# The S5 scan of a four-layer hybrid backbone: 32 groups per scan, products in PSUM, chunk states contiguous

## The chip, the cores and the metric

One core of a Trainium2 chip runs the whole program in one launch. The metric is the device time of a launch in microseconds (us). The engines go by short names: PE is TensorE's matmuls (PEld its weight loads), DVE is VectorE, ACT is ScalarE, POOL is GpSimd, SP issues most DMAs.

## The reference, cut to what matters

Four layers work on 384 tokens of width 1024 in float32: 128 context tokens and 256 latent tokens. Layers 0 and 3 mix tokens with S5, layer 1 with neighbourhood attention, layer 2 with grouped-query attention; every layer ends in a squared-ReLU MLP, and adaLN vectors modulate both halves of a layer. S5 works on 64 groups of 16 channels, with 64 complex states per group and direction:

```python
def s5_scan(ug, ar, ai, abr, abi, bbr, bbi, h0r, h0i, reverse):
    bur = jnp.einsum('gpk,blgk->blgp', bbr, ug)
    bui = jnp.einsum('gpk,blgk->blgp', bbi, ug)
    ...
    _, _, hr, hi = lax.associative_scan(s5_combine, (a_re, a_im, bur, bui), reverse=reverse, axis=1)
    # plus A^n h0 for the latent stream
def s5_mixer(...):
    for dr in range(2):
        hr, hi = s5_scan(ug, ..., reverse=(dr == 1))
        y = y + Re(C h)
        finals.append(the last state)
    z = jax.nn.gelu(y) @ glu_w + glu_b
    za, zg = jnp.split(z, 2, axis=-1)
    return za * jax.nn.sigmoid(zg), finals
```

The context stream starts from zero, the latent stream from `state_s5`; the context's last states are an output.

## The kernel before, in words

**Chunks.** Tokens are cut into 48 chunks of 8: 32 latent ones and 16 of the context. Both directions lie on the partitions: (direction, state) gives 128, and the backward half holds its chunks reversed. The 64 groups go through in 8 batches of 8 (`GB`). S5 has two passes over the batches.

**First pass** (`s5`, the loop over `b` with `s5_states`). For each batch, PE multiplies the chunks with the table E, ACT copies the sums (L1122), PE transposes them (L1129), and ACT copies them into the states' tile `s5s` (L1132 for the 32 latent chunks, L1133 for the 16 of the context). In layer 0 the table E is made on the spot (`make_e`): four DVE multiplications of 128x1024 per batch (`work<-tab,braw`), two POOL sums of 128x1024 (L823, L826), PE transposes. In layer 3 it comes from DRAM, where it was put beside the MLPs of earlier layers. Between the matmuls stand steps of adaLN (`fill`), as long as any are left.

**Scan** (`s5_scan`). After every `SG` = 16 groups, that is after two batches, the recurrence h[c] = A^8 h[c-1] + S[c] runs on DVE over the chunks: 32 steps, of which the first 16 advance both streams (two-stream steps) and the last 16 the latent stream alone (one-stream steps). Each step is three DVE instructions: `scm<-a,s5s` multiplies (128 wide, 64 in a one-stream step), `scm<-scm` adds the products' real and imaginary shares (64, 32), and `s5s<-scm,s5s` adds to S[c] in place (64, 32). Each waits for the one before it. A layer has four scans, each over its 16 groups. POOL copies the context's last states out (L1009).

**Second pass** (`s5_out`). Batch b needs the whole scan of its groups: ACT copies the state before each chunk into `hs` (L1162, four copies), PE multiplies with the table C (L1172) and the chunk's own inputs with the within-chunk table (L1169), ACT applies gelu (L1174). Every second batch, `turn` transposes the result (L1187) and splits it into two exact parts `k` (ACT L1190, DVE `k<-aux,k`). In layer 0 the table C is made here (`make_c`: four DVE multiplications `work<-tab,craw`, POOL sums L874, L877) in the buffers `whi` and `wlo` that otherwise hold weights; in layer 3 it is loaded (`ca`). From batch 4 on, the first half of the GLU's rows is multiplied too (`glu_first`, result `glupart`); after the last batch, `s5_glu` does the second half.

**What sets the order.** A scheduler reads the program and fixes the order of instructions on each engine; engines then run their lists in order and wait on semaphores. So an instruction that waits holds up all that stands behind it in its engine's list. [...]

Of the kernel before, what the change touches and what calls it, by code (L numbers as in the profile page):

```python
# [32 lines left out]
# S5: chunks of Q steps, NC chunk columns (latent 0-15, context 0-15, latent 16-31)  # L33
# [5 lines left out]
# groups per scan; output tiles of the GLU whose first half of the rows comes early  # L39
SG = 16  # L40
# [3 lines left out]
# batches of E and of C of the second S5 layer that are made beside the MLP of a layer  # L44
SPILL = {0: (0, 4), 1: (4, 2), 2: (4, 2)}
# steps of adaLN per step of S5, per projection of the neighbourhood and of the grouped-query attention
FS, FN, FG = 4, 2, 1
# steps of attention per projection
# [3 lines left out]
class Builder:  # L52
# [21 lines left out]
    def psum(self, mm, aux, tab=0, sc=0):  # L74
        """PSUM in banks: sums of projections, all else, tables and scores."""
        if self.ps:
            self.ps.close()
        self.ps = ExitStack()
        self.ps_mm = self.pool(self.ps, f"ps_mm{tab}", mm, space=PSUM)
        self.ps_aux = self.pool(self.ps, f"ps_aux{tab}", aux, space=PSUM)  # L80
        if tab:
            self.ps_tab = self.pool(self.ps, "ps_tab", tab, space=PSUM)
        if sc:
            self.ps_sc = self.pool(self.ps, "ps_sc", sc, space=PSUM)
# [29 lines left out]
    def setup(self):  # L114
# [29 lines left out]
        # the q gains carry the scales of the scores  # L144
# [4 lines left out]
    def streams(self, ap):  # L149
        """The two streams of [P, NTOK]: context columns, latent columns."""  # L150
        return (ap[:, 256:], ap[:, 0:256])

# [21 lines left out]
    def flush(self):  # L174
        """The end of the last group of ada()."""
# [55 lines left out]
    def split(self, pool, src, tag, bufs=None):  # L231
        """src as exact hi + lo."""
# [12 lines left out]
    def proj(self, src, x):  # L245
        """One output tile = chunk^T x over the 8 k-tiles of x."""
# [25 lines left out]
    def scratch(self, start, n):  # L272
        """n values of the space of the norm's parts, where they aren't in use."""
        return self.sc[:, start:start + n]

    def next_norm(self, l, n):
        """The norm that the residual stream goes to next, built up as its tiles become final."""
        self.nx = {"l": l, "n": n, "acc": None, "parts": None, "h": [], "s5": n == 0 and l % 3 == 0}

    def final(self, k):  # L280
        """x[k] is final: x gain as exact parts, the shifts in two more columns, or as chunks for S5; and the sum of
        squares."""
# [37 lines left out]
    def rstd(self):  # L320
        """1 / rms of every token, on all partitions."""
# [6 lines left out]
    def normed(self, pool, ps, r, func, dst):  # L328
        """dst = func(r * ps + shift) from a projection of the parts that final() makes."""
# [9 lines left out]
    def rsqrt(self, m, r):  # L339
        """(m + EPS)^-1/2: a first value from the tables, one Newton step."""  # L340
# [12 lines left out]
    def pick(self, out, gg, src):  # L353
        """out[(step, channel)] = src(step)[channel of group gg], steps in reverse."""
# [5 lines left out]
    def residual(self, ps, gate, f):  # L360
        """x[f] += gate * ps."""
# [3 lines left out]
    def out_proj(self, src, half, x, l, steps, fill):  # L365
        """x += gate * (W^T o) over half of the heads."""
# [64 lines left out]
    def head_rstd(self, pool, raws, kind):  # L431
        """1 / rms over the head dim of up to four raw [P, NTOK] tiles."""
# [9 lines left out]
    def head_norm(self, raw, r, j, gain, kind, t):  # L442
        """t = raw r gain, r that of the j-th tile."""
# [7 lines left out]
    def pipeline(self, items):  # L451
        """Pairs of functions, of which the first runs one ahead: steps that other work is interleaved with."""
# [7 lines left out]
    def steps(self, n):  # L460
        """n steps of the attention that runs beside the projections, and the fill of adaLN."""
# [11 lines left out]
    def value_flip(self, raws, v, first):  # L473
        """v[tok, t, feature] from features by tokens."""
# [3 lines left out]
    def softmax_tail(self, p, total):  # L478
        """p *= 1 / total."""
# [3 lines left out]
    def flip(self, p, n, dst):  # L483
        """dst[key, n, q] = transposes of p [q, n * P]."""
# [117 lines left out]
    def gqa(self, l):  # L602
        nc, i = self.nc, self.i
        with ExitStack() as ctx:
# [13 lines left out]
            def project(first, n, st):  # L618
                """The tiles of k (2) and q (8): projected, then normed, turned and used in steps."""
# [90 lines left out]
    def exp(self, pool, out, x):  # L710
        """exp(x) by 2^n e^r, x within float32's range of exponents."""
# [40 lines left out]
    def s5_tables(self, tp, wide, slot, pe, pc, a8):  # L752
        """Discretised parameters: powers of the step in the order of each direction, for E with B's factor; the matrix of
        Q steps. wide: space for 34 G values."""
# [21 lines left out]
        # f = (A - 1) / lambda  # L776
# [14 lines left out]
        # the order of the steps: the first 64 partitions run forward  # L791
# [16 lines left out]
    def make_e(self, pool, slot, b, pe, work, kf, kp, dd, et):  # L808
        """E[(step, channel), g, r, (direction, state)] = A^j B of GB groups, steps in reverse; and into DRAM the
        products Re(C A^j B) within a chunk, one row of 16 values per (distance, channel)."""  # L810
# [24 lines left out]
        # two groups per product, of which the diagonal blocks count  # L835
# [28 lines left out]
    def make_c(self, cr, b, pc, ca, t):  # L864
        """ca = (Re, -Im) of C A^j."""
# [13 lines left out]
    def s5_spill(self, slot, first, ebs, cbs):  # L879
        """The tables of a later S5 layer, kept in DRAM: steps that other work is interleaved with. The parameters come  # L880
        first, then E and C of some groups."""
# [55 lines left out]
    def s5(self, l, slot):  # L937
# [5 lines left out]
        # places in the scratch space: what final() makes, then the reversed chunks of the second half and y; sel;  # L943
        # the reversed chunks of the first half, then the states that y is made from; kp and d, or sums of states
# [5 lines left out]
        with ExitStack() as ctx:  # L950
# [3 lines left out]
            s = []  # L954
            for n in range(2):
                t = pool.tile([P, HG // SG, NC + 2, 2, SG], F32, name=f"s5s{n}", tag=f"s5s{n}")
                s += [t[:, m] for m in range(HG // SG)]
            for n, t in enumerate(s):
                nc.gpsimd.dma_start(t[:, 0], i["s5h0"][slot][:, :, n * SG:(n + 1) * SG])
                nc.gpsimd.memset(t[:, 33], 0.0)  # L960
# [24 lines left out]
            for b in range(NB):  # L985
# [20 lines left out]
                if not g:  # L1006
                    gg = slice((n - 1) * SG, n * SG)
                    self.s5_scan(pool, s[n - 1], a8[:, :, :, gg])
                    nc.gpsimd.tensor_copy(fin[:, :, gg], s[n - 1][:, NC + 1])  # L1009
# [49 lines left out]
    def s5_u(self, pool, u, make=None):  # L1059
        """u[(step, channel), g, chunk], steps in reverse: from x's chunks in layer 0, from those of x gain else."""  # L1060
# [45 lines left out]
    def s5_states(self, ssb, b, et, u, ur, s):  # L1106
        """S[c] = sum over the steps of a chunk of A^j B u for GB groups (columns 48-63 of a group belong to the next)."""
# [16 lines left out]
        def rest():  # L1124
            for n in range(GB // 4):
                pt = self.aux().rearrange("p (j r e c) -> p j r e c", r=2, e=2, c=CP)
                for j in range(2):
                    for r in range(2):
                        nc.tensor.transpose(pt[:, j, r].rearrange("p e c -> p (e c)"), sums[2 * n + j][:, r, :], self.ident[:])  # L1129
                for r in range(2):  # L1130
                    dst = s[:, :, r, gs + 4 * n:gs + 4 * n + 4].rearrange("p c (j e) -> p j e c", e=2)
                    nc.scalar.copy(dst[:, :, :, 1:33], pt[:, :, r, :, 0:32])  # L1132
                    nc.scalar.copy(dst[:, :, :, 34:], pt[:, :, r, :, 32:NC])  # L1133
        return rest

    def s5_scan(self, pool, s, a8):
        """h[c] = A^Q h[c - 1] + S[c] in place: the first value of each stream, then its chunks (latent from 0, context
        from 33); the backward half holds them in reverse."""
        w0 = s.shape[3]
        m = pool.tile([P, 2, 2, 2, w0], F32, name="scm", tag="scm", bufs=2)  # L1140
        for n in range(32):
            if n < 16:
                cur, prev = s[:, n + 1:n + 35:33], s[:, n:n + 34:33]
            else:
                cur, prev = s[:, n + 1:n + 2], s[:, n:n + 1]
            w = cur.shape[1]
            sh = [P, w, 2, 2, w0]
            self.mul(m[:, :w], a8.unsqueeze(1).to_broadcast(sh), prev.unsqueeze(2).to_broadcast(sh))
            self.add(m[:, :w, :, 0], m[:, :w, :, 0], m[:, :w, :, 1])
            self.add(cur, m[:, :w, :, 0], cur)  # L1150

    def s5_out(self, pool, b, ca, tz, u, s, hy, gsb, k):
        """The outputs of GB groups: from the state before each chunk and from the chunk itself."""
# [3 lines left out]
        for dr in range(2):  # L1157
            pp = slice(64 * dr, 64 * dr + 64)
            hv = hy[pp].rearrange("p g r c -> p c r g")
            for a0, n, src in ((0, 32, 0), (32, 16, 33)):  # L1160
                dst = hv[:, a0:a0 + n]
                nc.scalar.copy(dst if dr == 0 else dst[:, ::-1], sg[pp, src:src + n])  # L1162
# [32 lines left out]
    def glu_sums(self, slot, f, halves, k):  # L1195
        """Both output tiles of f over halves of the rows."""
# [181 lines left out]
```

## Time and profile before

| what | value |
|---|---|
| runs | 2102.32, 2106.98, 2116.06 us, median 2106.98 |
| span of the profiled execution | 2104.6 us |
| median minus that span | 2.4 us |
| busy: PE, DVE, ACT, POOL | 94%, 65%, 49%, 10% of the span |
| S5 of layer 0 | first output matmul at 149.8 us, last at 241.0 |
| S5 of layer 3 | first output matmul at 1714.4 us, last at 1778.0 |

The profiled execution has no time of its own beside the span; the runs' median lies 0.1% above it. In a list of groups, the first column is the source line; element-wise DVE instructions share the helper's line L93, so their tiles tell them apart. `128x64` is partitions by elements per partition. PEclk is the clock granted to PE, as a share of full speed.

### The profile page before, as it was taken

The page shows a single profiled execution, that of the slowest core. Times are in us where ns is not written, and L with a number is a line of the kernel's source. Part 1 is how long each engine was busy: PE and PEld are TensorE (multiplying, and loading weights), DVE is VectorE, ACT ScalarE, POOL GpSimd, SP SyncE. Part 2 cuts the span into 40 slices and gives each one's busy share as a digit, 9 for nine tenths or more (in the row PEclk, how much of TensorE's full clock was granted, in tenths as well). Part 3 has the DMA queues.
Part 4 walks back from the last instruction along what each step waited for, and adds up shares of the span by engine and source line. Part 5 has one row for each costly group of instructions (what it writes and reads, how often), then busy time and mean ns, then how long its engine had stood idle before and what let it go on. Part 6 is the DMA issues. An engine that isn't in the chain of part 4 may idle for free. (4 is left out here: it accounts for less than half of the span.)

```text
span 2104.6 us, 35187 instructions
## 1 busy us (share of the span) xinstructions
PE 1980.7 (94%) x13490; PEld 1747.3 (83%) x13490; DVE 1368.2 (65%) x3070; ACT 1029.4 (49%) x2112; POOL 216.4 (10%) x180
## 2 busy tenths in 40 slices
PE   5886899999999999999999999999999878999999
PEld 2554799999987777998999877998997657999999
DVE  7899669856445556856658566856665396674562
ACT  4664656335355555634435555534434477553441
POOL 4443210400000000001111000002111000000000
PEclk8997999999999999999999999999999999999999
DMA  7756654443365555634334532533444575333331
GB/s 286 234 199 238 233 182 152 152 170 120 128 233 192 177 179 193 230 121 154 125 132 163 172 114 98 179 131 128 142 149 156 165 281 221 121 126 125 124 131 67
DMA packets 130823, 348.45 MB, mean 166 GB/s; under 512 B 12800, under 2 KB 48544, under 8 KB 128608
## 3 DMA queue, kind: packets, MB, share of 16 engines
q1 hardware_dynamic: 124160, 338.55, 46.8%
q0 software_dynamic: 1712, 4.05, 0.6%
q10 hardware_dynamic: 4784, 3.61, 0.5%
q8 instruction: 107, 1.75, 0.3%
q14 instruction: 60, 0.49, 0.1%
HBM read 323.22 MB, written 22.94 MB: 164 GB/s over the span
## 5 line engine op out<-in xcount | busy, mean ns | idle before, releaser
L221 ACT CAST whi<-raw 128x1024 fp32r<-128x1024 f32 x340 | 356.4, 1049 | 486.4 <-PE mm L228 422.6
L93 DVE TENSOR_TENSOR wlo<-raw,whi 128x1024 fp32r<-128x1024 f32 x340 | 445.2, 1310 | 197.2 <-ACT whi L221 196.3
L227 PE MATMUL mm<-h,whi 128*128 128x386 f32 x1312 | 453.4, 346 | 0.0
L229 PE MATMUL mm<-h,wlo 128*128 128x386 f32 x1312 | 448.2, 342 | 0.0
L228 PE MATMUL mm<-h,whi 128*128 128x386 f32 x1312 | 446.9, 341 | 0.0
L227 PE MATMUL mm<-ahi,whi 128*128 128x384 f32 x1024 | 350.2, 342 | 10.3 <-ACT ahi L235 10.3
L229 PE MATMUL mm<-ahi,wlo 128*128 128x384 f32 x1024 | 349.3, 341 | 2.8 <-DVE wlo L93 2.8
L228 PE MATMUL mm<-alo,whi 128*128 128x384 f32 x1024 | 349.8, 342 | 1.7 <-DVE alo L93 1.6
L227 PEld LDWEIGHTS mm<-h,whi 128*128 128x128 f32 x1312 | 246.7, 188 | 21.7 <-issue 16.7
L228 PEld LDWEIGHTS mm<-h,whi 128*128 128x128 f32 x1312 | 248.3, 189 | 5.0 <-issue 3.7
L229 PEld LDWEIGHTS mm<-h,wlo 128*128 128x128 f32 x1312 | 247.4, 189 | 5.3 <-issue 4.0
L111 DVE SCALAR_TENSOR_TENSOR x<-mm,mod,x 128x128 f32<-128x128 f32 (+1 forms) x256 | 95.4, 412 | 204.8 <-PE mm L229 204.3
L227 PEld LDWEIGHTS mm<-ahi,whi 128*128 128x128 f32 x1024 | 195.3, 191 | 13.3 <-ACT ahi L235 12.6
L229 PEld LDWEIGHTS mm<-ahi,wlo 128*128 128x128 f32 x1024 | 195.3, 191 | 5.0 <-DVE wlo L93 3.4
L228 PEld LDWEIGHTS mm<-alo,whi 128*128 128x128 f32 x1024 | 195.2, 191 | 5.1 <-DVE alo L93 5.1
L163 PE MATMUL ada<-raw,silu 128*2 128x256 f32 x1536 | 127.1, 407 | 21.1 <-DMA raw<-in_ada_w 16.5
L93 DVE TENSOR_TENSOR nt<-mm,rstd 128x384 f32<-128x384 f32 x164 | 90.6, 553 | 68.1 <-PE mm L229 67.5
L337 ACT ACTIVATE relu<-nt,nb 128x128 f32<-128x128 f32 (+1 forms) x256 | 102.1, 447 | 46.3 <-DVE nb L335 45.9
L235 ACT CAST ahi<-asq 128x384 fp32r<-128x384 f32 x128 | 65.4, 513 | 119.2 <-DVE asq L93 118.8
L93 DVE TENSOR_TENSOR alo<-asq,ahi 128x384 fp32r<-128x384 f32 x128 | 73.0, 572 | 50.3 <-ACT ahi L235 50.2
L163 PEld LDWEIGHTS ada<-raw,silu 128*2 128x2 f32 x1536 | 31.4, 85 | 77.4 <-issue 32.2
L227 PE MATMUL mm<-k,whi 128*128 128x384 f32 x256 | 89.1, 352 | 6.0 <-DVE k L93 2.1
(376 smaller groups left out, 3019.1 us busy)
## 6 DMA issues: line engine op xcount, KB each, us to landing
raw<-in_w SPq DMA_DIRECT2D x256, 512.0 KB, 3.5
raw<-in_ada_w SPq DMA_DIRECT2D x192, 512.0 KB, 4.7
raw<-in_glu SPq DMA_DIRECT2D x32, 512.0 KB, 5.5
tz<-kdr SPq DMA_DIRECT2D x16, 512.0 KB, 5.8
dca<-ca SPq DMA_DIRECT2D x8, 1024.0 KB, 4.3
raw<-in_na_wqk SPq DMA_DIRECT2D x16, 512.0 KB, 4.1
det<-et SPq DMA_DIRECT2D x32, 256.0 KB, 2.6
et<-det SPq DMA_DIRECT2D x32, 256.0 KB, 5.7
```

Source lines behind the costliest of these rows:

```text
L93: self.nc.vector.tensor_tensor(out, a, b, op=op)
L111: self.nc.vector.scalar_tensor_tensor(out, a, s, b, op0=op0, op1=op1)
L163: nc.tensor.matmul(ps[32 * j:32 * j + 2], self.silu[:, k, :], raw[:, 256 * j:256 * j + 256], start=(k == 0), stop=(k == KT - 1))
L221: nc.scalar.copy(hi[:], raw[:])
L227: mm(out, whi, xhi, start=first, stop=False)
L228: mm(out, whi, xlo, start=False, stop=False)
L229: mm(out, wlo, xhi, start=False, stop=last)
L235: self.nc.scalar.copy(hi[:], src)
L337: nc.scalar.activation(o, z, func, bias=b[:, s:s + 1])
```

## The change

`SG` goes from 16 to 32: a layer has two scans of 32 groups, the first after batch 3, the second after batch 7. Each step still has three DVE instructions, of twice the width. The multiplication (256 wide, 128 in a one-stream step) writes its products to a PSUM bank `m`, which the scan keeps to its end; two additions (128, 64) then take the products' two shares from PSUM one after the other and add each straight to S[c] in SBUF. In layer 3 `m` is an `sc` bank; in layer 0 the first scan takes one of the three `aux` banks, the second one of the two `mm` banks. The 48 chunks lie at 0 to 47 of the states' tile and the two start values at 48 and 49, so that a batch's S come in by two ACT copies (L1129, 128x384) in place of eight, and leave `s5_out` by five copies (64x752, 64x496, 64x240 and two of 64x32) in place of four. The copy of the last context states, L1008, still needs only the first 16 steps. Four DMAs and four memsets of start values on POOL, ahead of S5, go.

```diff
-SG = 16
+SG = 32
...
-            s = []
-            for n in range(2):
-                t = pool.tile([P, HG // SG, NC + 2, 2, SG], F32, name=f"s5s{n}", tag=f"s5s{n}")
-                s += [t[:, m] for m in range(HG // SG)]
+            s = [pool.tile([P, NC + 2, 2, SG], F32, name=f"s5s{n}", tag=f"s5s{n}") for n in range(2)]
             for n, t in enumerate(s):
-                nc.gpsimd.dma_start(t[:, 0], i["s5h0"][slot][:, :, n * SG:(n + 1) * SG])
-                nc.gpsimd.memset(t[:, 33], 0.0)
+                nc.gpsimd.dma_start(t[:, NC], i["s5h0"][slot][:, :, n * SG:(n + 1) * SG])
+                nc.gpsimd.memset(t[:, NC + 1], 0.0)
...
-                    self.s5_scan(pool, s[n - 1], a8[:, :, :, gg])
-                    nc.gpsimd.tensor_copy(fin[:, :, gg], s[n - 1][:, NC + 1])
+                    m = self.scores() if sp else (self.aux, self.mm_tile)[n - 1]()
+                    self.s5_scan(m, s[n - 1], a8[:, :, :, gg])
+                    nc.gpsimd.tensor_copy(fin[:, :, gg], s[n - 1][:, NC - 1])
...
-                pt = self.aux().rearrange("p (j r e c) -> p j r e c", r=2, e=2, c=CP)
+                pt = self.aux().rearrange("p (r j m) -> p r j m", r=2, m=P)
...
-                for r in range(2):
-                    dst = s[:, :, r, gs + 4 * n:gs + 4 * n + 4].rearrange("p c (j e) -> p j e c", e=2)
-                    nc.scalar.copy(dst[:, :, :, 1:33], pt[:, :, r, :, 0:32])
-                    nc.scalar.copy(dst[:, :, :, 34:], pt[:, :, r, :, 32:NC])
+                nc.scalar.copy(s[:, 0:NC, :, gs + 4 * n:gs + 4 * n + 4].rearrange("p c r g -> p r g c"),
+                               pt.rearrange("p r j (e c) -> p r (j e) c", c=CP)[:, :, :, 0:NC])
...
-        m = pool.tile([P, 2, 2, 2, w0], F32, name="scm", tag="scm", bufs=2)
+        m = m[:, :8 * SG].rearrange("p (w a r g) -> p w a r g", a=2, r=2, g=SG)
         for n in range(32):
...
             self.mul(m[:, :w], a8.unsqueeze(1).to_broadcast(sh), prev.unsqueeze(2).to_broadcast(sh))
-            self.add(m[:, :w, :, 0], m[:, :w, :, 0], m[:, :w, :, 1])
-            self.add(cur, m[:, :w, :, 0], cur)
+            for r in range(2):
+                self.add(cur, m[:, :w, :, r], cur)
...
-            for a0, n, src in ((0, 32, 0), (32, 16, 33)):
-                dst = hv[:, a0:a0 + n]
-                nc.scalar.copy(dst if dr == 0 else dst[:, ::-1], sg[pp, src:src + n])
+            if dr == 0:
+                nc.scalar.copy(hv[:, 1:NC], sg[pp, 0:NC - 1])
+            else:
+                nc.scalar.copy(hv[:, 30::-1], sg[pp, 0:31])
+                nc.scalar.copy(hv[:, 46:31:-1], sg[pp, 32:47])
+            first, gap = ((0, 32), (31, 16))[dr]
+            nc.scalar.copy(hv[:, first:first + gap + 1:gap], sg[pp, NC:NC + 2])
```

In the changed kernel the lines move a little: the copies into the states' tile are L1129, those out of it L1155 to L1160, the output matmuls L1167 and L1170, gelu L1172.

**DVE, layer 3, kernel before**, where the first scan of a tile has reached its one-stream steps. `s5s_16539` is the tile that holds the first two scans; a width of 2x32 is a two-stream step, 32 a one-stream step.

```order
L93 TENSOR_TENSOR scm<-a_16550,s5s_16539 128x128
L93 TENSOR_TENSOR s5s_16539<-scm,s5s_16539 128x2x32
L93 TENSOR_TENSOR scm<-scm 128x4x16
L93 TENSOR_TENSOR scm<-a_16550,s5s_16539 128x64
L93 TENSOR_TENSOR s5s_16539<-scm,s5s_16539 128x2x32
L93 TENSOR_TENSOR scm<-scm 128x2x16
L93 TENSOR_TENSOR scm<-a_16550,s5s_16539 128x128
L93 TENSOR_TENSOR s5s_16539<-scm,s5s_16539 128x32
```

**The same place in the changed kernel.** `s5s_16299` holds the first scan (batches 0 to 3), `s5s_16300` the second (4 to 7); `x2` is the two additions of a step.

```order
L93 TENSOR_TENSOR sc<-a_16306,s5s_16299 128x256
L93 TENSOR_TENSOR s5s_16299<-sc,s5s_16299 128x2x64 x2
L93 TENSOR_TENSOR s5s_16300<-sc,s5s_16300 128x2x64
L93 TENSOR_TENSOR sc<-a_16306,s5s_16299 128x128
L93 TENSOR_TENSOR s5s_16300<-sc,s5s_16300 128x2x64
L93 TENSOR_TENSOR s5s_16299<-sc,s5s_16299 128x64
L93 TENSOR_TENSOR sc<-a_16306,s5s_16300 128x256
L93 TENSOR_TENSOR s5s_16299<-sc,s5s_16299 128x64
```

In both, two scans alternate. Before, these are scans over batches 0 and 1 and over 2 and 3. In the changed kernel the first scan's 16 two-stream steps stand by themselves (the first two rows repeat), then the second scan's first addition, which needs the copies of batch 7 among others, stands ahead of the first scan's 16 one-stream steps, and the two alternate from there.

**ACT, layer 3, changed kernel**, from the copies of the last two batches to the first gelu.

```order
L1129 COPY s5s_16300<-aux 128x2x4x48
L1158 COPY hs<-s5s_16299 64x15x2x8
L221 CAST whi<-raw 128x1024 x4
L1157 COPY hs<-s5s_16299 64x31x2x8 x2
L1155 COPY hs<-s5s_16299 64x47x2x8 x2
L1160 COPY hs<-s5s_16299 64x2x2x8 x2
L1172 ACT_TABLE_LOAD
L1172 ACTIVATE hs<-aux 128x4x8x16
```

The copies out of the states' tile that need the end of the first scan (L1157 and L1155, of batches 0 and 1) stand after the last copy into it; before, six copies out of it (L1162) stood ahead of the last batch's copies into it.

**DVE, layer 0, changed kernel**, where the first scan starts. `work<-tab,braw` is E, `mod` adaLN; `aux` holds the products.

```order
L93 TENSOR_TENSOR work<-tab,braw 128x1024 x13
L93 TENSOR_TENSOR mod_2_975<-aux,ab 128x8 x2
L93 TENSOR_TENSOR work<-tab,braw 128x1024 x8
L93 TENSOR_TENSOR aux<-a_159,s5s_148 128x256
L93 TENSOR_TENSOR s5s_148<-aux,s5s_148 128x2x64 x2
```

Before, a first scan started after batch 1, with E's multiplications between its steps. Now 28 of the 32 multiplications of E stand ahead of the first scan; the other four and ten of the table C's stand among its steps, and the second scan begins in the first one's eighth one-stream step.

## Rows read from the trace of the kernel before

**Rows 1.** the page, engines: busy us (share of the span) and instructions

```profile
PE 1980.7 (94%) x13490; PEld 1747.3 (83%) x13490; DVE 1368.2 (65%) x3070; ACT 1029.4 (49%) x2112; POOL 216.4 (10%) x180
```

**Rows 2.** windows, layer 0: window, its us, busy us by engine, PEclk, DMA

```profile
100.00:125.00 25.00, 21.27 (x244) 12.59 (x230) 25.00 (x93) 16.85 (x57) 9.69 (x9) 1.00 0.62 223
...
175.00:200.00 25.00, 14.14 (x122) 8.35 (x122) 25.00 (x76) 6.42 (x14) 10.42 (x7) 0.66 0.59 205
200.00:225.00 25.00, 21.05 (x203) 17.52 (x204) 23.22 (x58) 15.09 (x26) 9.60 (x4) 0.93 0.74 247
```

**Rows 3.** windows, layer 3, columns as in rows 2

```profile
1714.30:1731.00 16.70, 11.40 (x155) 9.58 (x154) 14.53 (x88) 14.79 (x21) 0.21 (x1) 0.95 0.76 268
1731.00:1743.00 12.00, 9.19 (x68) 7.43 (x68) 9.20 (x59) 3.86 (x7) 0.68 (x2) 0.78 0.51 186
1743.00:1767.00 24.00, 23.81 (x204) 22.36 (x205) 17.37 (x62) 19.68 (x26) 0.08 (x1) 0.93 0.67 258
1767.00:1782.00 15.00, 12.05 (x113) 9.64 (x110) 4.43 (x12) 8.50 (x23) 0.00 (x0) 1.00 0.55 199
```

**Rows 4.** groups, VectorE, 97.5 to 235 us: shapes, count | busy us, mean ns

```profile
L93 DVE TENSOR_TENSOR work<-tab,craw 128x1024 f32<-128x1024 f32 x32 | 38.7, 1213 | 0.8 <-PE aux L1172 0.5 <-issue 0.3
L93 DVE TENSOR_TENSOR scm<-a,s5s 128x64 f32<-128x64 f32 x64 | 25.8, 421 | 0.2
L93 DVE TENSOR_TENSOR scm<-scm 128x32 f32<-128x32 f32 x64 | 25.6, 406 | 0.1
L93 DVE TENSOR_TENSOR scm<-a,s5s 128x128 f32<-128x128 f32 x57 | 18.7, 356 | 0.0
L93 DVE TENSOR_TENSOR s5s<-scm,s5s 128x32 f32<-128x32 f32 x64 | 11.5, 183 | 0.1
...
L93 DVE TENSOR_TENSOR k<-aux,k 128x192 fp32r<-128x192 f32 x12 | 6.1, 510 | 0.0
...
L93 DVE TENSOR_TENSOR mod<-aux,ab 128x8 f32<-128x8 f32 x12 | 1.9, 159 | 0.0
L111 DVE SCALAR_TENSOR_TENSOR gain<-mod,ng 128x8 f32<-128x8 f32 x4 | 0.6, 160 | 0.0
```

**Rows 5.** groups, GpSimd, 0 to 260 us, columns as in rows 4

```profile
L874 POOL TENSOR_TENSOR work<-work 128x1024 f32<-128x1024 f32 x8 | 19.1, 2391 | 34.5 <-DVE work L93 19.4 <-DVE s5s L93 10.0 <-DVE scm L93 5.1
```

**Rows 6.** timeline, VectorE, layer 0: start us, us, line, operation, tiles

```profile
112.13 2.58 DVE L93 TENSOR_TENSOR scm<-a,s5s 128x64 f32<-128x64 f32 x2
```

**Rows 7.** timeline, GpSimd, the same stretch

```profile
112.12 2.45 POOL L823 TENSOR_TENSOR work<-work 128x1024 f32<-128x1024 f32 x1 [3.06 <-DVE s5s L93]
```

**Rows 8.** timeline, VectorE, layer 3, two-stream steps (at the end: idle before, releaser)

```profile
1690.28 0.29 DVE L93 TENSOR_TENSOR scm<-a,s5s 128x128 f32<-128x128 f32 x1
1690.61 0.22 DVE L93 TENSOR_TENSOR scm<-scm 128x64 f32<-128x64 f32 x1
...
1691.62 0.23 DVE L93 TENSOR_TENSOR s5s<-scm,s5s 128x64 f32<-128x64 f32 x1 [0.20 <-ACT s5s L1133]
1691.76 0.22 DVE L93 TENSOR_TENSOR scm<-scm 128x64 f32<-128x64 f32 x1
```

**Rows 9.** timeline, VectorE, layer 3, one-stream steps of the last scan alone

```profile
1757.57 0.19 DVE L93 TENSOR_TENSOR scm<-scm 128x32 f32<-128x32 f32 x1
...
1760.64 0.19 DVE L93 TENSOR_TENSOR s5s<-scm,s5s 128x32 f32<-128x32 f32 x1
```

**Rows 10.** timeline, ScalarE, layer 3, around the first output

```profile
1713.73 0.36 ACT L1133 COPY s5s<-aux 128x64 f32<-128x64 f32 x1
1714.12 2.25 ACT L1162 COPY hs<-s5s 64x512 f32<-64x512 f32 x2
```

**Rows 11.** output matmuls, layer 3: ns min/median/max, first and last start us

```profile
L1172 PE MATMUL aux<-ca,hs x256: 272/273/450, 1714.4 to 1778.0; 128*48 128x128 f32 x128
```

**Rows 12.** output matmuls, layer 0, columns as in rows 11

```profile
L1172 PE MATMUL aux<-work,hs x256: 272/273/448, 149.8 to 241.0; 128*48 128x128 f32 x128
```

**Rows 13.** timeline, ScalarE, layer 0, end of the copies of batch 3

```profile
97.49 0.32 ACT L1133 COPY s5s<-aux 128x64 f32<-128x64 f32 x1
```

More of the change, by code (lines that the diff above doesn't have):

```diff
@@ L1125, in rest, with s5_scan @@
             for n in range(GB // 4):
-                pt = self.aux().rearrange("p (j r e c) -> p j r e c", r=2, e=2, c=CP)
+                pt = self.aux().rearrange("p (r j m) -> p r j m", r=2, m=P)
                 for j in range(2):
                     for r in range(2):
-                        nc.tensor.transpose(pt[:, j, r].rearrange("p e c -> p (e c)"), sums[2 * n + j][:, r, :], self.ident[:])
-                for r in range(2):
-                    dst = s[:, :, r, gs + 4 * n:gs + 4 * n + 4].rearrange("p c (j e) -> p j e c", e=2)
-                    nc.scalar.copy(dst[:, :, :, 1:33], pt[:, :, r, :, 0:32])
-                    nc.scalar.copy(dst[:, :, :, 34:], pt[:, :, r, :, 32:NC])
-        return rest
-    def s5_scan(self, pool, s, a8):
-        w0 = s.shape[3]
-        m = pool.tile([P, 2, 2, 2, w0], F32, name="scm", tag="scm", bufs=2)
+                        nc.tensor.transpose(pt[:, r, j], sums[2 * n + j][:, r, :], self.ident[:])
+                nc.scalar.copy(s[:, 0:NC, :, gs + 4 * n:gs + 4 * n + 4].rearrange("p c r g -> p r g c"),
+                               pt.rearrange("p r j (e c) -> p r (j e) c", c=CP)[:, :, :, 0:NC])
+        return rest
+    def s5_scan(self, m, s, a8):
+        m = m[:, :8 * SG].rearrange("p (w a r g) -> p w a r g", a=2, r=2, g=SG)
         for n in range(32):
[L1142 to L1147, printed above, removed]
+            w = 2 if n < 16 else 1
+            at = lambda c: s[:, c:c + 32 * w - 31:32] if w > 1 else s[:, c:c + 1]
+            cur, prev = at(n), at(n - 1) if n else s[:, NC:NC + 2]
+            sh = [P, w, 2, 2, SG]
             self.mul(m[:, :w], a8.unsqueeze(1).to_broadcast(sh), prev.unsqueeze(2).to_broadcast(sh))
-            self.add(m[:, :w, :, 0], m[:, :w, :, 0], m[:, :w, :, 1])
-            self.add(cur, m[:, :w, :, 0], cur)
+            for r in range(2):
+                self.add(cur, m[:, :w, :, r], cur)
     def s5_out(self, pool, b, ca, tz, u, s, hy, gsb, k):
```

## The prediction

> **What bounds the kernel now.** The page's engines come first: PE is busy for 94% of the span, DVE for 65% [rows 1]. So a DVE saving counts only in a stage where PE waits for DVE. S5 is the only part that the change touches, so the next view is the windows of its two layers. In layer 0 DVE is busy for 25.00 us of 25 in four windows from 100 to 200 us, of which the first and last stand here, while PE falls to 14.14 of 25 at a granted clock of 0.66 [rows 2]: this stage is bound by DVE. In layer 3 PE is busy for 11.40 + 9.19 + 23.81 + 12.05 = 56.5 us of the 67.7 us from the first output matmul, at 1714.4, to 1782 [rows 3, 11]; 11.2 us are gaps. The groups on DVE in layer 0 say what fills it: scans, then the tables of C, 32 x 1.21 us [rows 4]. The timelines then give the price of one step of a scan [rows 8, 9] and what releases the first output [rows 10].
>
> **Instructions of a scan.** A step's three instructions wait for each other, so a scan alone pays each duration and a gap: 1690.28 + 0.29 = 1690.57, and the next starts at 1690.61, a gap of 0.04; where two scans alternate, the next starts after 0.14 (1691.62 to 1691.76) although 0.23 is its duration, that is 0.08 to 0.09 earlier than it ends [rows 8]. Durations: 128 wide 0.29, 64 wide 0.22 [rows 8], 32 wide 0.19 [rows 9]. From 64 to 128 is 1.1 ns an element, so I estimate 0.43 for 256 wide. Per 32 groups:
> - before, two scans alternating: two-stream pair of steps 2 x (0.21 + 0.14 + 0.14) = 0.98, one-stream 2 x (0.14 + 0.11 + 0.11) = 0.72; 16 of each, 27 us.
> - after, hidden among other work: 0.35 + 2 x 0.21 = 0.77 and 0.21 + 2 x 0.14 = 0.49; 16 of each, 20 us.
> - after, alone: 0.47 + 2 x 0.33 = 1.13 and 0.33 + 2 x 0.26 = 0.85; 16 of each, 32 us.
>
> So the change saves 7 us of DVE per 32 groups where other work fills the gaps, and costs 5 where nothing does. What fills them is the order of the instructions.
>
> **The PSUM operand.** No row shows DVE writing to PSUM. A read from PSUM costs nothing in the nearest row, `mod<-aux,ab` at 159 ns against 160 for `gain<-mod,ng` from SBUF; the far end is `k<-aux,k`, 510 ns at 192 wide where 64 and 128 wide at 0.22 and 0.29 would give 0.36, so 0.15 dearer [rows 4, 8]. I take nothing, by the short instructions, which are nearest in length; nothing excludes a gain, which I bound by the surplus below. [...]
>
> **Layer 3.** Before, the first scans were long done when batch 7's copies into the states ended (1713.73 + 0.36 = 1714.09), and the first output matmul came at 1714.4 [rows 10, 11]. Now:
> - The first scan starts when batch 3's copies are in, as before at 1691.62, where DVE's idle time ends on ACT's copy [rows 8]. Its 16 two-stream steps stand alone: 16 x 1.13 = 18, to 1709.6.
> - The second scan's first addition stands next in DVE's list and waits for batch 7's copies. Two copies in place of eight save ACT under 1 us, so about 1713.
> - 16 steps of both, 0.49 + 0.77 = 1.26 each, 20 us: the first scan ends at 1733.
> - ACT's copies out follow. Two of 64x512 took 2.25 [rows 10], so by size 64x496 takes about 1.1 and 64x752 about 1.65; two of L1157 and two of L1155 (5.5) stand ahead of the first small one. Output starts at about 1738.
>
> That is 24 us later than 1714.4, and PE has nothing else in its list there. Part of it comes back: before, PE waited on later scans (the last ended at 1760.64 + 0.19 [rows 9]), now the second ends at 1733 + 16 x 0.85 = 1747, ahead of the output that needs it. PE's 56.5 us of work [rows 3] put the end at 1794.5 without a gap, 12.5 after 1782, and at 24 later with all gaps kept. The idle stretch may lower PE's clock, which stood at 0.78 behind the gaps of 1731 to 1743 [rows 3], and a stretch without gaps may raise it, so I count neither. I take +13: the gaps were waits for scans and copies, and these are over by then.
>
> **Layer 0.** DVE's list is shorter. The scans' instructions are lengthened here: one-stream multiplications take 421 ns in place of 220 and first additions 406 in place of 190, two-stream multiplications 356 in place of 290 [rows 4, 8, 9]: 64 x 0.20 + 64 x 0.22 + 57 x 0.07 = 31 us. Where from: a pair of multiplications takes 2.58 us from 112.13 to 114.71 while POOL's sum runs from 112.12 to 114.57 [rows 6, 7]. The tables of C, with one source in PSUM, stay at 1213, and POOL's sums take 2.39 [rows 4, 5]. After, the additions have one source in PSUM, and only the multiplications have two in SBUF; since DVE works in order, POOL's sum may still catch the next multiplication. I keep half of the 31, and bound it by none and by all. So DVE saves 2 x 7 + 15 = 29 us at best, and about 25 with some steps alone.
>
> Against it stands the late start. Batch 3's copies end at 97.81 [rows 13], and 28 tables of E stand ahead of the first scan, so I start it at 102. 16 steps of 1.13, eight other tables (9.7, which fill some gaps) and 8 us of POOL lead to about 137; eight one-stream steps, six tables and 4 us of POOL (0.85 x 8 + 7.3 + 4 = 18) to 155; eight joint steps of 1.26 to 165. With copies out, output starts at about 167 against 149.8 [rows 12]. Then DVE has left the rest of the second scan (7 x 0.9 + 16 x 0.6 = 16), 22 tables (25, at 1.14 start to start), POOL 8, and the rest 10: 59, to 226, and about 7 more to the last output matmul: 233 against 241.0 [rows 12]. PE's own work in that stretch is, by the mean of the last two windows (17.6 of 25) [rows 2], 64 of its 91 us, so its floor is 167 + 64 = 231. I take -4, half of the 8, since neither engine will go without gaps. The two held PSUM banks make `aux` two for batches 4 to 7, and `mm` one until the second scan ends; the GLU, which needs both `mm`, starts after that anyway. I price them at nothing, at up to +8 for the range (2 us for each of four batches).
>
> **The sum.** 2104.6 (the profiled span) + 13 - 4 = 2113.6; the median lies 2.4 above the span, so **2116**. The ACT copies saved and the DMAs on POOL lie beside other work; if ACT were on the path in the first pass, they would give 1 us a batch.
>
> **The rivals.**
> - *Forecast* (0.50): layer 3 pays, layer 0 gives a little back: 2103 to 2127.
> - *Layer 0 gains fully* (0.22). The stall goes with the products, DVE loses all 31 us, the first scan ends ten earlier, and and PE's floor is 157 + 64 = 221: -20 at most, -15 with some gaps. Layer 3 still pays 6 to 13: 2093 to 2105; were it to pay nothing, 2085 to 2092. For it: DVE's full windows and the 2.58 us [rows 2, 6]. Against: the multiplications keep two SBUF sources.
> - *Late outputs pass through* (0.20), slower. The mechanism is layer 3's first scan, which ends only after batch 7's copies: where the gaps of 11.2 us return behind the late start (copies out of ACT being the pace, five a batch in place of four), the delay of 24 stays, layer 0 gives 0: 2131. It decides from 19 us net on. For it: PE's list holds nothing else meanwhile. Against: the last scan, which ended at 1760.83, is over sooner [rows 9].
> - *PSUM operands dearer* (0.08): by the far end of 0.15, 48 + 96 instructions with one in layer 3's path add up to 20 us there, of which half may come back, and 10 in layer 0: 2126 to 2146.
>
> About 1% (21 us) is what a measurement here can tell from no change. Below 2086: the low case of layer 0's full gain with nothing paid in layer 3, 0.10. Above 2128: most of the third and half of the last, 0.22. Within: 0.68. The range leaves out one tenth at each side: 2092 to 2134.
>
> **What would show it.** In the profile after: L1129's last copy in layer 3 at about 1713 and the first output matmul at 1738 on the old time axis, with PE empty between; the first scan's steps at 1.1 us alone and 1.26 in pairs; PE nearly full from then on. In layer 0: additions from PSUM near 0.22 and 0.29 without a long tail, multiplications with a tail up to 2.4; first output at 160 to 170, last at 230 to 240. Wrong would be: additions from PSUM above 0.35, a first output in layer 3 before 1730, or an output in layer 0 after 245.

## The result

The changed kernel takes 2124.57 us (median of 4 runs, 2122.01 to 2130.14), the kernel before 2107.07 on the same chip: a ratio of 1.0088, 95% interval 1.0066 to 1.0109. It is 17.5 us slower. The forecast was 2116 in a range of 2092 to 2134.

The page's line of engines, which answers to [rows 1]: DVE lost 38 us of busy time, and the program got longer.

```profile
PE 1974.4 (93%) x13490; PEld 1735.5 (82%) x13490; DVE 1330.2 (63%) x2686; ACT 1032.1 (49%) x2032; POOL 212.2 (10%) x168
```

**Where the time went.** All kernels here cast 340 weight chunks in the same order (`whi<-raw`), so the starts of these casts divide a profile into stages: to the 9th cast (layer 0's S5), to the 257th (the middle layers), to the 281st (layer 3's S5). From there to the last cast it is 249.0 us in every kernel, and to the end 269.8. "First output" is the time from the start of layer 3's stage to its first output matmul. Each number below is read from the trace of the one profiled execution.

| kernel | layer 0 | middle | layer 3: first output | layer 3 whole |
|---|---|---|---|---|
| before | 258.4 | 1343.0 | 113.1 | 233.5 |
| changed | 257.0 | 1341.7 | 132.5 | 253.5 |

Layer 0 gave 1.4 us, the middle 1.3, and layer 3 took 20.0, on spans of 2104.6 and 2122.0.

**Layer 3.** Output matmuls of the changed kernel (first and last start), against 1714.4 and 1778.0 in [rows 11]; the stage began 2.7 us earlier:

```profile
L1170 PE MATMUL aux<-ca,hs x256: 272/273/450, 1731.2 to 1794.8; 128*48 128x128 f32 x128
```

The windows ahead of the first output and behind it (columns as in [rows 3]): PE is empty for 22.5 us, then busy for 55.52 of 67.8 us, where [rows 3] have 56.5 of 67.7. PE's granted clock stands at its lower level (0.50) in the hole, yet behind it the mean is 0.91, against 0.92 by the windows of [rows 3].

```profile
1708.70:1731.20 22.50, 0.02 (x2) 0.03 (x2) 22.50 (x102) 9.19 (x11) 0.85 (x2) 0.50 0.27 109
1731.20:1799.00 67.80, 55.52 (x533) 49.12 (x533) 24.39 (x68) 42.74 (x76) 0.00 (x0) 0.91 0.57 195
```

The waits of PE between 1700 and 1800 (total, times, longest) name a single one for that hole; `L1160` is the last of the copies out of the states' tile:

```profile
PE aux L1170 <- ACT hs L1160: 22.5, 1, 22.5
PE aux L1185 <- DVE s5s L93: 5.7, 1, 5.7
```

Two timelines, DVE and then ACT, show what the copies waited for. The first scan's two-stream steps alone start 1.11 us apart (1687.69 to 1688.80: a multiplication of 0.43, two additions in 0.62). They end at 1704.41. DVE then idles 3.81 us for batch 7's copies, which end at 1708.18, and the joint steps follow at 1.20 us each (1709.61 to 1710.81).

```profile
1687.69 0.43 DVE L93 TENSOR_TENSOR sc<-a,s5s 128x256 f32<-128x256 f32 x1
1688.15 0.62 DVE L93 TENSOR_TENSOR s5s<-sc,s5s 128x128 f32<-128x128 f32 x2
1688.80 0.43 DVE L93 TENSOR_TENSOR sc<-a,s5s 128x256 f32<-128x256 f32 x1
...
1703.79 0.62 DVE L93 TENSOR_TENSOR s5s<-sc,s5s 128x128 f32<-128x128 f32 x2
1708.21 0.29 DVE L93 TENSOR_TENSOR s5s<-sc,s5s 128x128 f32<-128x128 f32 x1 [3.81 <-ACT s5s L1129]
...
1709.61 0.29 DVE L93 TENSOR_TENSOR sc<-a,s5s 128x128 f32<-128x128 f32 x1
...
1710.81 0.29 DVE L93 TENSOR_TENSOR sc<-a,s5s 128x128 f32<-128x128 f32 x1
```

```profile
1707.38 0.80 ACT L1129 COPY s5s<-aux 128x384 f32<-128x384 f32 x1
...
1726.27 1.92 ACT L1157 COPY hs<-s5s 64x496 f32<-64x496 f32 x2 [10.90 <-DVE s5s L93]
1728.21 2.85 ACT L1155 COPY hs<-s5s 64x752 f32<-64x752 f32 x2
```

The copies out start at 1726.27, when the first scan's last step but one is done, and 4.9 us later PE starts.

**Layer 0.** Output matmuls, against 149.8 and 241.0 in [rows 12], the scans' groups from 97.5 to 235 us, against [rows 4], and two windows, against [rows 2]:

```profile
L1170 PE MATMUL aux<-work,hs x256: 272/273/421, 164.4 to 241.2; 128*48 128x128 f32 x128
```

```profile
L93 DVE TENSOR_TENSOR aux<-a,s5s 128x256 f32<-128x256 f32 x16 | 11.2, 700 | 0.4
L93 DVE TENSOR_TENSOR mm<-a,s5s 128x256 f32<-128x256 f32 x16 | 10.2, 640 | 0.0
L93 DVE TENSOR_TENSOR mm<-a,s5s 128x128 f32<-128x128 f32 x16 | 9.5, 595 | 0.4
L93 DVE TENSOR_TENSOR s5s<-aux,s5s 128x128 f32<-128x128 f32 x32 | 9.3, 289 | 1.3 <-ACT s5s L1129 0.4
...
L93 DVE TENSOR_TENSOR s5s<-aux,s5s 128x64 f32<-128x64 f32 x32 | 6.8, 212 | 0.2
L93 DVE TENSOR_TENSOR aux<-a,s5s 128x128 f32<-128x128 f32 x16 | 6.6, 413 | 0.1
```

```profile
150.00:175.00 25.00, 16.66 (x211) 9.22 (x205) 19.72 (x65) 15.32 (x22) 6.59 (x3) 0.80 0.91 312
...
200.00:225.00 25.00, 13.78 (x155) 10.17 (x154) 13.82 (x35) 10.86 (x17) 2.35 (x1) 0.80 0.62 207
```

The scans are much cheaper: with the two groups of `mm` additions left out here (8.9 and 7.1 us) they are busy for 69.6 us; four of the six groups before alone took 81.6 [rows 4]. Additions with one source in PSUM stay at 289 and 212 ns; the multiplications, with two in SBUF, are lengthened, at 700 ns where layer 3's take 430. DVE, full in all of 100 to 200 us before, now has gaps. Yet output starts 14.6 us later and ends at 241.2.

### The profile page after: what moved, and what is told of

It reads as the page before. It is cut to its first block, busy times and chain, and to the rows that moved or that the text cites. A ratio compares the mean times of both kernels' runs of the same rounds, so it can differ in the third digit from the quotient of the medians.

```text
span 2122.0 us, 34660 instructions
## 1 busy us (share of the span) xinstructions
PE 1974.4 (93%) x13490; PEld 1735.5 (82%) x13490; DVE 1330.2 (63%) x2686; ACT 1032.1 (49%) x2032; POOL 212.2 (10%) x168
## 5 line engine op out<-in xcount | busy, mean ns | idle before, releaser
L163 PE MATMUL ada<-raw,silu 128*2 128x256 f32 x1536 | 133.1, 414 | 39.0 <-DMA raw<-in_ada_w 25.3
## 6 DMA issues: line engine op xcount, KB each, us to landing
det<-et SPq DMA_DIRECT2D x32, 256.0 KB, 2.7
et<-det SPq DMA_DIRECT2D x32, 256.0 KB, 5.7
```

Of the source, the lines that this page charges most:

```text
L163: nc.tensor.matmul(ps[32 * j:32 * j + 2], self.silu[:, k, :], raw[:, 256 * j:256 * j + 256], start=(k == 0), stop=(k == KT - 1))
```

## The experiments

Ratios are to the kernel before, in runs on the same chip. The stages of all experiments, in us:

| kernel | ratio (95% interval) | layer 0 | middle | layer 3: first output | layer 3 whole |
|---|---|---|---|---|---|
| l0_32 | 1.0027 (1.0009 to 1.0046) | 254.5 | 1345.9 | 115.2 | 238.4 |
| l3_32 | 1.0152 (1.0125 to 1.0179) | 266.4 | 1348.4 | 133.0 | 255.2 |
| both16 | 1.0079 (1.0049 to 1.0108) | 264.8 | 1346.2 | 115.4 | 238.4 |
| sbuf | 1.0128 (1.0100 to 1.0155) | 264.0 | 1342.1 | 129.9 | 251.5 |
| share3 | 1.0115 (1.0094 to 1.0136) | 257.5 | 1354.0 | 128.4 | 253.1 |
| old32 | 1.0055 (1.0036 to 1.0075) | 253.2 | 1347.2 | 129.6 | 249.4 |
| layout16 | 1.0051 (1.0033 to 1.0069) | 261.9 | 1346.6 | 113.6 | 238.6 |
| mix | 0.9998 (0.9979 to 1.0017) | 257.2 | 1348.2 | 110.7 | 229.8 |
| tail_cut | 1.0104 (1.0086 to 1.0122) | 256.7 | 1345.0 | 133.7 | 253.2 |
| ada_after | 1.0115 (1.0095 to 1.0135) | 254.6 | 1344.6 | 131.4 | 253.7 |
| ada_before | 1.0022 (1.0008 to 1.0036) | 256.0 | 1340.1 | 110.1 | 237.8 |
| ada_mix | 1.0043 (1.0026 to 1.0060) | 258.8 | 1342.6 | 108.0 | 237.4 |

The same code of a stage differs by up to 4 us between kernels in layer 0 (254.5 to 258.8 in the six other kernels that have the changed kernel's layer 0) and in layer 3 (233.5 before, 229.8 in mix), and by more in the middle, where none of these kernels is changed (the last section has the reason). So stages are compared, and differences under 4 us are not read.

### Which layer, and is it the grouping

**l0_32**, 32 groups in layer 0 only (`SGS` gives the groups for layers 0 and 3; the edits here are cut to the lines that matter):

```diff
-SG = 32
+SGS = (32, 16)
```

> Two scans of 32 groups in layer 0, four of 16 in layer 3; products in PSUM and the contiguous layout in both. Theory A (layer 3's late first output is the whole loss): layer 3 comes back to its time before, so 2100 to 2108 us, within 0.4% of the kernel before. Rival B (the loss is in what both layers share: PSUM products, five copies out in place of four): about half of the 17 us stays, 2113 to 2118.

2114.3 us, ratio 1.0027. Theory A and rival B each hold in part: 15 of layer 3's 20 us are gone, but it stays 5 above the kernel before.

**l3_32**, 32 groups in layer 3 only. In layer 0 two scans of 16 share a PSUM bank, one half each:

```diff
-SG = 32
+SGS = (16, 32)
...
-                    m = self.scores() if sp else (self.aux, self.mm_tile)[n - 1]()
+                    if sp:
+                        m = self.scores()
+                    elif SG == 32:
+                        m = (self.aux, self.mm_tile)[n - 1]()
+                    elif n % 2:
+                        bank = (self.aux, self.mm_tile)[n // 2]()
+                        m = bank
+                    else:
+                        m = bank[:, 256:]
```

> Four scans of 16 groups in layer 0, two of 32 in layer 3; products in PSUM and the contiguous layout in both. Theory A: layer 3 starts its output some 22 us late as in the changed kernel and ends about 20 late, layer 0 is at or below its time before, so 2115 to 2127 us. Rival B: half the loss, 2113 to 2118, with layer 0 losing as much as layer 3.

2141.5, outside what either theory gave. Layer 3's loss is 22 us, as theory A has it; the surprise is layer 0, at 266.4, 8 us worse than before and some 10 worse than with 32 groups.

**both16**, with `SGS = (16, 16)` and the same banks:

> Four scans of 16 groups in both layers, products in PSUM, contiguous layout. Theory A (grouping alone costs): no loss; layer 3 -3 us by the fewer copies in, layer 0 -3 to -12 as additions from PSUM no longer wait for GpSimd: 2092 to 2104 us. Rival B (PSUM and layout cost): slower than before by 8 us or more.

2126.2: theory A fails for the whole kernel, and the time is where rival B put it. Layer 3 has the 5 us again, first output 2 us late and the rest slower. PE's wait ahead of the first output ends on a copy out of the states, which had no such share before:

```profile
PE aux L1183 <- ACT hs L1173: 4.3, 1, 4.3
```

In layer 0 the trace shows the two scans of a bank one after the other: the first one's last multiplication starts at 129.1 us, the second one's first at 130.0, where the kernel before ran such scans side by side. That is likely a cost of this kernel's own way to place products; layout16 (below), which does not share banks, has 261.9 in layer 0, so it is not shown to be all of the 6 to 8 us.

**layout16**, 16 groups with products in SBUF, three instructions of `scm` as before, only the new layout:

```diff
-SG = 32
+SGS, PSM, OLD, SHARE = (16, 16), (0, 0), (False, False), (0, 0)
...
+                    if not PSM[slot]:
+                        m = pool.tile([P, 8 * SG], F32, name="scm", tag="scm", bufs=2)
...
+            if not direct:
+                self.add(m[:, :w, :, 0], m[:, :w, :, 0], m[:, :w, :, 1])
+                self.add(cur, m[:, :w, :, 0], cur)
+                continue
```

(By layer: `PSM`, products in PSUM, which `s5_scan` gets as `direct`; `OLD`, the old layout; `SHARE`, one bank for both scans.)

> Four scans of 16 groups, products in SBUF as before, and only the contiguous layout with its two copies in and five copies out. Theory F: layer 3 ends 4 to 5 us late by the copies out, layer 0 about as before: 2110 to 2116 us. Rival G (the layout also costs layer 0 its 7 us, and not the bank that two scans shared in the kernel with 16 groups and PSUM products): 2118 to 2128.

2120.1, in rival G's range, but the stages do not bear G out: layer 0 is 3.5 above before, within what is not read, and not 7; the unchanged middle adds 3.6. Layer 3 is again at 238.6, so the 5 us there belong to the layout and not to PSUM. In the three kernels of 16 groups with the new layout, PE's clock stands at its lower level for 15.1 to 19.2 us behind layer 3's first output, before for 10.2; half of the difference, 2.5 to 4.5 us, is about what that part lost (2.5 to 4.6).

**old32**, 32 groups and PSUM products with the old layout: eight copies in, four out.

```diff
-SG = 32
+SGS, PSM, OLD, SHARE = (32, 32), (1, 1), (True, True), (0, 0)
...
+            if self.old:
+                cur, prev = (s[:, n + 1:n + 35:33], s[:, n:n + 34:33]) if w > 1 else (s[:, n + 1:n + 2], s[:, n:n + 1])
```

> As the changed kernel (32 groups, products in PSUM), but with the old layout of the states: eight copies in, four copies out. Theory F (the five copies out cost some 4 us before the first output in layer 3, as the gap of 4.3 us in the two kernels of 16 groups there): 2118 to 2123 us. Rival: the layout changes nothing, as copies in are dearer by as much: 2123 to 2128.

2121.5: theory F's range. Layer 3 is 4.1 shorter than in the changed kernel. Together with the three kernels of 16 groups, the layout costs 4 to 5 us in layer 3, the grouping 15 to 16 (249.4 against 233.5). With mix's 229.8 (below) for the old layer 3 it is up to 9 and up to 20.

**mix**, layer 0 as changed, layer 3 wholly as before:

```diff
-SG = 32
+SGS, PSM, OLD, SHARE = (32, 16), (1, 0), (False, True), (0, 0)
```

> Layer 0 as in the changed kernel, layer 3 wholly as in the kernel before. Theory A: layer 0 gives 1 to 4 us, layer 3 nothing: ratio to before 0.998 to 1.000, 2102 to 2108 us, against the rival that what layer 0 saves is lost to drift in the later layers: 1.000 to 1.003.

2107.0, ratio 0.9998 (0.9979 to 1.0017). All of the loss is gone, and no gain from layer 0 can be told.

### PSUM

**sbuf**, the changed kernel with its products in SBUF:

```diff
-                    m = self.scores() if sp else (self.aux, self.mm_tile)[n - 1]()
+                    m = pool.tile([P, 8 * SG], F32, name="scm", tag="scm", bufs=2)
```

> As the changed kernel (32 groups), but the products lie in SBUF. Theory A: layer 3 as in the changed kernel; in layer 0 additions have two SBUF sources again and the surplus of some 14 us on the multiplications grows to 20 to 30 over all three instructions; as VectorE has gaps there now, only part shows: 2124 to 2135 us. Rival C (PSUM operands are dearer than SBUF ones): faster than the changed kernel by 5 us or more, below 2119.

2136.0, 1.0128 against 1.0088: 1 us above theory A's range, and rival C falls. The groups from 97.5 to 235 us:

```profile
L93 DVE TENSOR_TENSOR s5s<-scm,s5s 128x128 f32<-128x128 f32 x64 | 25.7, 402 | 1.9 <-ACT s5s L1129 0.9
L93 DVE TENSOR_TENSOR s5s<-scm,s5s 128x64 f32<-128x64 f32 x64 | 21.6, 338 | 1.3
```

The same additions took 289 and 212 ns from PSUM (278 and 221 for the second scan). In layer 3, where POOL has no such work (from 1680 to 1765 it is busy for 1.1 us in the changed kernel), the 128-wide additions take 0.29 us from SBUF, too, and the time is not longer (251.5). Layer 0 of the changed kernel shows the two kinds beside POOL's sums: a 256-wide multiplication with both sources in SBUF takes 2.24 us in place of 0.43 from 108.02, where `L826` runs from 107.60 for 2.36 us, and an addition from PSUM takes 0.28 at 106.43, inside `L823`'s 2.38 from 105.27; none of the 128 additions from PSUM takes more than 293 ns. That the longer additions of sbuf lie beside POOL's sums is the author's inference from this and from [rows 6, 7]; the rows of sbuf are means. So PSUM products are worth some 5 to 9 us in layer 0 (264.0 against 254.5 to 258.8), where POOL's sums run beside the scans, and nothing in layer 3.

### Why the delay in layer 3 was not made up

**share3**, layer 3's second scan uses the first one's bank, and so waits for its end:

```diff
-SG = 32
+SGS, PSM, OLD, SHARE = (32, 32), (1, 1), (False, False), (0, 1)
...
+                    elif SHARE[slot] and n > 1:
+                        pass
+                    else:
+                        m = self.scores() if sp else (self.aux, self.mm_tile)[n - 1]()
```

> As the changed kernel, but in layer 3 both scans use one PSUM bank for their products, so the second scan cannot start before the first has ended, and the first one's one-stream steps no longer stand behind an addition that waits for batch 7. Theory D (half of layer 3's delay is that wait and the alternation): the first scan ends at about 1717, the first output comes some 8 to 10 us earlier than in the changed kernel's 1731, and the end 5 to 9 us earlier: ratio to before 1.004 to 1.007, 2115 to 2120 us. Rival E (the second scan's end or the pace of the copies sets the end anyway): within 3 us of the changed kernel, 2122 to 2127.

2133.7, above what either gave. The first output comes 4.1 us earlier in its stage, half of what theory D said, but layer 3 ends where it did (253.1): rival E there. The second scan now runs alone and ends at 1782.5, so that the outputs of batch 4 start at 1785.6. The output matmuls, first and last start:

```profile
L1202 PE MATMUL aux<-ca,hs x256: 272/273/449, 1740.0 to 1807.9; 128*48 128x128 f32 x128
```

What the whole kernel lost is in the middle layers, at 1354.0, where it was not changed.

**tail_cut**, the second scan of layer 3 without its last 16 steps, so that the latent states of batches 4 to 7 stay unfinished:

```diff
-                    self.s5_scan(m, s[n - 1], a8[:, :, :, gg])
+                    self.s5_scan(m, s[n - 1], a8[:, :, :, gg], 16 if sp and n == 2 else 32)
```

> As the changed kernel, but layer 3's second scan leaves out its last 16 steps (the latent states of batches 4 to 7 are unfinished). The first scan and the first output stay where they are, about 1731. Theory H (part of the delay is not made up because the subtractions of k, and output 4, stand behind the second scan's tail on VectorE): the 5.7 us gap of TensorE after output 3 goes, and the end comes 5 to 9 us earlier than in the changed kernel, 2116 to 2120 us. Rival I (the 22 us delay is kept by what TensorE itself has left, and by ScalarE's copies): within 3 us, 2122 to 2127.

2127.3: rival I. The windows before and behind the first output, and PE's waits behind it:

```profile
1713.10:1735.50 22.40, 0.03 (x1) 0.00 (x0) 22.40 (x97) 9.06 (x11) 1.79 (x2) 0.50 0.27 104
1735.50:1803.00 67.50, 56.99 (x534) 49.80 (x534) 13.80 (x26) 41.84 (x76) 0.00 (x0) 0.92 0.56 195
```

```profile
PE aux L1185 <- DVE k L93: 5.3, 2, 4.2
PE mm L227 <- ACT k L1188: 2.3, 4, 0.6
PE aux L1185 <- ACT hs L1172: 1.5, 1, 1.5
PE aux L1167 <- DMA tz<-kdr: 1.0, 1, 1.0
```

DVE has 13.80 us of work left, against 24.39 in the changed kernel, and PE still takes 67.5 us for 57 of its own. Of the 10.5 us of gaps, 7.6 end on the subtraction or the cast of k. The gap after the first two outputs stays: it is 4.2 in place of 5.7 us. It ends on a subtraction of k on DVE, which waits for a cast on ACT. In the changed kernel ACT's list at that point (timeline) has the copies of the next batches ahead of the cast (L1188); in tail_cut's list it stands three copies earlier.

```profile
1738.51 1.03 ACT L1157 COPY hs<-s5s 64x496 f32<-64x496 f32 x1
...
1740.44 0.60 ACT L1158 COPY hs<-s5s 64x240 f32<-64x240 f32 x1
...
1741.12 1.45 ACT L1155 COPY hs<-s5s 64x752 f32<-64x752 f32 x1
...
1743.89 0.60 ACT L1158 COPY hs<-s5s 64x240 f32<-64x240 f32 x1
1744.52 0.50 ACT L1188 CAST k<-aux 128x192 fp32r<-128x192 f32 x1
```

**ada_after**, the changed kernel with no adaLN in layer 3's first pass, so that 32 steps come in the second:

```diff
-                self.fill(FS)
+                self.fill(0 if sp else FS)
                 rest()
```

> As the changed kernel, but layer 3's first pass holds no steps of adaLN; 32 of them, some 9 us of TensorE and 128 matmuls, come in the second pass, where TensorE waits. Theory J (the delay costs because TensorE has nothing else in its list there): the copies of batches 3 and 7 come 3 to 9 us earlier, and the end 5 to 12 us earlier than in the changed kernel: 2112 to 2120 us. Rival (the moved steps collide with the outputs or with loads): 2122 to 2130.

2131.2: theory J fails, and the time is 1 us above the rival's range. The first output moves by 1.1 us and the hole grows, since PE is done with the first pass sooner and only 32 matmuls of adaLN, behind its start, stand ahead of the first output in its list:

```profile
PE aux L1170 <- ACT hs L1160: 27.1, 1, 27.1
```

**ada_before** and **ada_mix**, the same line in the kernel before and in mix:

> The kernel before with the same move of adaLN's steps in layer 3. Theory J: there TensorE's gaps in the second pass are 11 us in all, each 1 to 2 us, so 0 to 6 us are to be had: 2101 to 2107 us against 2107 to 2110 for the kernel before. Rival: the same time or slower, as loads of adaLN weights collide with C's tables.

> Layer 0 of the changed kernel, layer 3 of the kernel before, and the move of adaLN's steps in layer 3. If layer 0's small gain and that of the move add up: ratio 0.995 to 0.999 to the kernel before, 2098 to 2106 us. Rival: no difference, 0.999 to 1.002.

2113.1 (1.0022) and 2114.2 (1.0043): no gain, ada_mix slower than its rival's 1.002. First outputs come 3 us earlier (110.1 and 108.0 against 113.1 and 110.7), and the stage is 4 to 8 us longer, so the steps seem to cost more in the second pass than in the first. No version beats the kernel before.

## Why the prediction was right, and where it was off

The direction, the range and the likeliest case held; the size was half of what was measured (+9 on the spans, 13 less 4, against +17.4). That the likeliest case held is in part luck: in layer 3 the delay was 19.4 us where 24 were forecast, and nothing of it came back where 11 were, and these two errors have opposite signs.

- *The price of a step.* Forecast 1.13 us alone and 1.26 joint, measured 1.11 and 1.20. The 256-wide multiplication was put at 0.43 and took 0.43.
- *PSUM operands at nothing.* Held: in layer 3, two additions of 128 take 0.62 us from PSUM, as from SBUF by [rows 8] with a gap, and 0.29 us each from SBUF in sbuf. The means of the 64-wide additions to `s5s` in layer 3 (1680 to 1765) agree: 217 ns from PSUM in the changed kernel, 220 from SBUF before. And sbuf is slower, not faster: 1.0128 against 1.0088.
- *Half of the surplus behind POOL stays.* Forecast 15 of 31 us. Measured over 430 and 290 ns: 16 x (0.27 + 0.21) + 16 x (0.31 + 0.12) = 14.6.
- *Layer 0.* First output forecast at 167, was 164.4; the last at 233 to 237, was 241.2. The stage gained 1.4 where 4 was forecast, and runs of the same code lie further apart than that. (In the second rival's price 2085 should be 2087, which changes no reading here.) That DVE's saving was lost to the late start is what the first output and DVE's gaps show, no experiment separates it.
- *Layer 3's late output.* 24 us forecast, 22.5 us of hole and 19.4 later within the stage (the stage's first pass was a little faster, by batch 7's copies at 1708.18, some 3 earlier within it). Its mechanism held in all its steps: lone steps, a wait for batch 7, joint steps, copies out.
- *The term that failed: "+13: the gaps were waits for scans and copies, and these are over by then."* From the first output to the end of the stage the kernel before takes 120.4 us, the changed one 121.0, tail_cut 119.5, old32 119.8, mix 119.1. PE's gaps (11.2 us before, 12.3 in the changed kernel) are not waits for scans: 10.5 us are there in tail_cut, where DVE is busy for 13.80 of 67.5 us. The trace before had it already. Of PE's waits from 1714.5 to 1782, only 1.3 us end on copies out of the states. The largest share, 3.6 us, are two waits of transposes. The row names s5s, the addition that DVE runs right behind a subtraction of k; for these two subtractions DVE itself had waited 2.17 and 2.79 us, until ACT's cast:

```profile
PE aux L1187 <- DVE s5s L93: 3.6, 2, 2.2
PE aux L1169 <- ACT hs L1162: 1.1, 1, 1.1
```

```profile
1739.49 0.50 DVE L93 TENSOR_TENSOR k<-aux,k 128x192 fp32r<-128x192 f32 x1 [2.79 <-ACT k L1190]
```

  What these waits name is the chain of transpose, cast and subtraction that each pair of outputs goes through, with ACT's copies in between. That this chain sets the length is read from the waits; no run takes it out. PE's clock, which was not counted, is no rival: behind the first output it stands at its lower level for 11.8 us, before for 10.2, which is 0.8 us of work. So nothing of the delay returns, PE is not "nearly full from then on", and the term is +20. With it the sum is 2104.6 + 20 - 4 + 2.4 = 2123. This was the third rival (0.20), in its price of layer 3 and in the gaps that return; its reason, five copies out in place of four, is not borne out: old32, with four, takes 119.8.
- *The copies* were counted as neutral. The new layout costs 4 to 5 us of layer 3's 20, in four kernels that agree, on one profiled execution each; which of the copies it is was not tried.

## What to carry to other kernels

A wider instruction was cheaper per element (0.29 us for a multiplication of 128, 0.43 for 256), but a scan over twice the groups starts after twice the batches, and layer 3's first output came 19.4 us later: price the first result's delay, not only the engine's time. Before crediting a stage with making up a delay, ask what its gaps wait for; the chain of short hand-overs between three engines took as long when it started late (121.0 us against 120.4). Moving one source of an addition to PSUM paid only where GpSimd worked beside it: layer 0 took 264.0 us in sbuf against 254.5 to 258.8, layer 3 took 251.5 against 253.5.

## What was not expected of the hardware

share3 has the same instruction order as the changed kernel up to layer 3, yet its middle layers took 12 us more. Two windows of the changed kernel and the same of share3 show PE's granted clock falling below full speed in one and not in the other:

```profile
670.00:705.00 35.00, 34.21 (x225) 26.16 (x224) 20.00 (x60) 20.88 (x52) 1.08 (x2) 1.00 0.58 199
790.00:825.00 35.00, 34.69 (x227) 26.04 (x229) 23.84 (x89) 17.74 (x58) 1.62 (x3) 1.00 0.61 203
```

```profile
670.00:705.00 35.00, 33.48 (x204) 24.82 (x204) 18.16 (x53) 18.08 (x44) 1.08 (x2) 0.90 0.59 189
790.00:825.00 35.00, 33.45 (x214) 25.59 (x213) 21.63 (x75) 16.34 (x48) 1.62 (x3) 0.95 0.61 200
```

In share3 PE waited 1.5 us ahead of each fall, in the changed kernel 0.8 us or less at the same instructions. These two windows account for some 5 us of the 12 (an estimate: 10% of 35 us and 5% of 35 us). The clock accounts for the rest, too: summed over the middle layers, it stands at its lower level, half of full speed (PEclk 0.50), for 10.2 us in the changed kernel and for 35.4 us in share3. Half of the difference is 12.6 us, and 12.3 were lost. Over all 14 kernels the middle runs from 1340.1 to 1354.0 us; less half of the time at the lower level it runs from 1333.6 to 1338.1. So most of what differs between kernels in this unchanged part goes with the clock. Why share3's waits were longer stays open.
